# Logits of the latent-attention layer: two heads at a time, the rotary parts in four quadrants of the array

## The chip, the cores and the metric

The kernel runs on one core of a Trainium2 chip. The metric is the device time of one execution in microseconds, as the median of repeated runs; for the kernel before it is 2040.04 us (three runs, 2040.04 to 2044.45). The profile is taken in an execution of its own.

## The reference, cut to what matters

Four layers follow each other on 256 tokens of width 2048: a state-space layer, an attention layer with forget gates ("fox"), a latent-attention layer ("mla") and a second state-space layer ("s5"). The change is in the third one:

```python
def mla_mixer(h, positions, w_in, q_norm, kv_norm, w_q_up, w_kv_up, w_out):
    ...
    q = (rms_norm(q_lat, q_norm) @ w_q_up).reshape(bsz, T, H, MLA_NOPE + MLA_ROPE)     # 16 heads, 128 + 64
    kv = (rms_norm(kv_lat, kv_norm) @ w_kv_up).reshape(bsz, T, H, MLA_NOPE + MLA_V)    # 16 heads, 128 + 128
    ...
    q = jnp.concatenate([q[..., :MLA_NOPE], q_pe], axis=-1)
    k = jnp.concatenate([kv[..., :MLA_NOPE], jnp.broadcast_to(k_pe[:, :, None, :], ...)], axis=-1)
    o = causal_block_attention(q, k, kv[..., MLA_NOPE:], (MLA_NOPE + MLA_ROPE) ** -0.5)
    y = o.reshape(bsz, T, MLA_WIDTH) * jax.nn.silu(z)
    return y @ w_out
```

A head's logits are a sum over 192 features: 128 that each head has for itself (the long product) and 64 rotary ones, whose keys all heads share. With 256 tokens, causal, there are three blocks of 128 x 128: queries 0-127 with keys 0-127, queries 128-255 with keys 128-255, and queries 128-255 with keys 0-127.

## The kernel before, in words

Weights come in half tiles by DMA into seven `raw` buffers (L108). ScalarE rounds each to a high part (`whi`, L119), VectorE makes the rest (`wlo`, L120), four buffers of each, and TensorE multiplies in three products (L126 to L128 with the tokens in rows, L212 to L214 with the features in rows). Such a step takes 12 products of L126 to L128 or 24 of L212 to L214, and ends with `C.tick()`, which runs what is due in a queue: `C.defer(n, fn)` puts `fn` n ticks ahead, and what becomes due is issued behind the step's last product.

The third layer's attention goes over four groups of four heads. A group makes the queries `qs` (line `mla_qn`, two steps), the keys `ks` (`mla_kn`, two steps) and the values `V` (two steps) of its four heads. Between them the queue brings the heads' softmax: `soft` of head c comes 1 + c ticks behind the keys; its `turn` (the transposes of the probabilities, L436, tile `pT`) two ticks later, and its `values` (L444, L445, tile `o`) one tick after that. `soft` calls `logits`: for each of the three blocks d the long product (L897: 128 features of the head) and the 64-row product (L898: rows 0-63 or 64-127 of `qpe` and `kpe`, by the head's parity) into one of four auxiliary PSUM banks, tile `lps`. VectorE evicts it with scale and mask (L900, L902, tile `lg`), takes the maxima (L415, L416) and the negated maxima (L422); ScalarE makes the exponentials (L425, L426, tile `pr`); VectorE divides (L428 to L430). Matrix products are of type float32, each of them two instructions on TensorE; `lg` has two buffers.

Two other places serve for comparison. The second layer's logits (L726 to L728) are three long products per head without a rotary part. The last layer sends 64x64 products into quadrants of the array: L1287 and L1399 use four quadrants in turn, L1383 two.

Of the kernel before, what the change touches and what calls it, by code (L numbers as in the profile page):

```python
# [11 lines left out]
F32 = mybir.dt.float32  # L12
# [3 lines left out]
ALU = mybir.AluOpType  # L16
# [3 lines left out]
P = 128  # L20
# [759 lines left out]
def mla(C, hT, out):  # L780
    nc, A = C.nc, C.A
    H, R, NR = 16, 64, 512
    mm = nc.tensor.matmul
    with C.tc.tile_pool(name="mla", bufs=1) as mp, C.tc.tile_pool(name="mla_w", bufs=1) as wp, C.tc.tile_pool(name="mla_t", bufs=2) as tp:
        C.lt = tp
        mask = C.causal(mp)
# [72 lines left out]
        kpe = mp.tile([P, T], F32, name="kpe")  # L859
# [15 lines left out]
        qpe = mp.tile([P, 8, T], F32, tag="lat", name="qpe")  # L875
        for s in range(2):
            ps = C.proj_tok([A["mla_qr"][s, 0]], latT[0])
            for t in range(2):
                qr = tp.tile([P, 8, R], F32, tag="qr", name="qr")
# [6 lines left out]
        yT = C.new_hT()  # L886
        sc = (P + R) ** -0.5

        def head(h, q, k, V):
            b = 64 * (h % 2)  # L890
            qr, kr_ = qpe[b:b + 64, h // 2], kpe[b:b + 64]

            def logits():
                lps = C.aux("lps")
                for d, qt, kt in ((0, 0, 0), (1, 1, 1), (2, 1, 0)):
                    o, a, e = lps[:, d * P:(d + 1) * P], slice(qt * P, (qt + 1) * P), slice(kt * P, (kt + 1) * P)
                    mm(o, q[:, a], k[:, e], start=True, stop=False)  # L897
                    mm(o, qr[:, a], kr_[:, e], start=False, stop=True)  # L898
                lg = tp.tile([P, 384], F32, tag="lg", name="lg")
                nc.vector.scalar_tensor_tensor(lg[:, 0:256], lps[:, 0:256], sc, mask.rearrange("p a b -> p (a b)"),  # L900
                                               op0=ALU.mult, op1=ALU.subtract)
                nc.vector.tensor_scalar(lg[:, 256:384], lps[:, 256:384], sc, None, op0=ALU.mult)  # L902
                return lg

            def finish(o):
                y = tp.tile([P, T], F32, tag="yf", name="yf")
                nc.vector.scalar_tensor_tensor(y, o[:, 0:T], 0.5, zs[h], op0=ALU.mult, op1=ALU.mult)
                C.split(yT[0][h], yT[1][h], y)

            return C.attend(logits, lambda: V[0], h % 4, finish)  # L910

        for g in range(4):
            qs, ks, Vs = [], [], []
            for nm, l, dst in (("mla_qn", 0, qs), ("mla_kn", 1, ks)):
                for c, ps in enumerate(C.proj_Tk([A[nm][g, 0]], latT[l])):
                    s = tp.tile([P, T], F32, tag=nm, name=nm, bufs=5)
                    nc.scalar.copy(s, ps)
                    dst.append(s)
            for c in range(4):
                C.defer(1 + c, head(4 * g + c, qs[c], ks[c], Vs))  # L920
            V = wp.tile([P, 2, 512], F32, tag="Vg", name="Vg", bufs=2)
            Vs.append(V)
            for t, ps in enumerate(C.proj_tok([A["mla_v"][g, 0]], latT[1])):
                nc.scalar.copy(V[:, t], ps)
# [540 lines left out]
SCAN_US = 1.9  # L1465
LAT_STRIPS = (364, 362, 362)
LAYERS = {0: ssd, 1: fox, 2: mla, 3: s5}


# [99 lines left out]
```

## Time and profile before

| | us |
|---|---|
| median of three runs | 2040.04 |
| the profiled execution | 2042.04 |
| its span on the core | 2040.2 |
| TensorE busy | 1988.5 |
| VectorE busy | 1472.4 |
| ScalarE busy | 957.6 |

The profile comes from one execution. The busy time of an engine is the union of its instructions' spans; a matrix product's span goes on until its result is through, so the spans overlap, and the time from one start (or end) to the next tells what a product costs. The chain of waits lists each piece by the time that it adds behind the piece before.

### The profile page before, as it was taken

To read this page: it belongs to the slowest core of one execution; us is meant where nothing else is said; L and a number is where in the kernel's file an instruction comes from. 1 tells how busy PE (TensorE), PEld (TensorE's weight loads), DVE (VectorE), ACT (ScalarE), POOL (GpSimd) and SP (SyncE) were. 2 spreads that over 40 slices of the span, in tenths; PEclk is the share of its full clock that TensorE was granted. 3 is DMA by queue.
4 is the path that set the end of the run, shared out by engine and by line. 5 is a ranking of instruction groups with operands and counts; after the bars stand their busy time and mean duration, and the time that the engine had idled before them with its cause. 6 is when DMAs were issued, how large, how long until landed. Compare 5 with 4: busy or idle time off the path is not lost.

```text
span 2040.2 us, 31823 instructions
## 1 busy us (share of the span) xinstructions
PE 1988.5 (97%) x12073; PEld 1695.5 (83%) x12073; DVE 1472.4 (72%) x2572; ACT 957.6 (47%) x1427; POOL 409.7 (20%) x482
## 2 busy tenths in 40 slices
PE   8999999999999999999999999999999999999997
PEld 6788888888888878788888879888888799778885
DVE  6798887887644695677776567766556678996856
ACT  5455555555433334344444444545554355445542
POOL 0101111001100018999991000000000000110002
PEclk9999999999999999999999999999999999999999
DMA  8555555555665547565666555654347556685652
GB/s 285 186 184 181 185 176 184 186 185 185 218 200 191 181 139 242 182 205 198 197 209 197 180 183 150 205 190 145 104 145 252 174 184 197 171 250 194 196 191 91
DMA packets 116233, 382.40 MB, mean 187 GB/s; under 512 B 18208, under 2 KB 20976, under 8 KB 114288
## 3 DMA queue, kind: packets, MB, share of 16 engines
q1 hardware_dynamic: 103424, 348.11, 52.5%
q0 software_dynamic: 7808, 26.56, 4.2%
q10 hardware_dynamic: 4848, 5.70, 0.8%
q8 instruction: 95, 1.56, 0.3%
q14 instruction: 58, 0.48, 0.1%
HBM read 366.20 MB, written 14.11 MB: 186 GB/s over the span
## 4 chain that ended last, share of the span: by engine, by line
PE 82%; DVE 10%; DMA 3%; POOL 2%; issue 2%; ACT 1%; SPq 0%; DVEq 0%; POOLq 0%; ACTq 0%
PE pT L147 24%; PE pT L148 12%; PE pt L127 10%; PE pt L126 10%; PE pt L128 10%; DVE wlo L120 3%; PE pk L212 2%; PE pk L214 2%; PE pk L213 2%; PE yd L602 1%; PE lps L898 1%; PE lps L897 1%; DVE hres L339 1%; DVE hres L340 1%; PE o L444 1%
## 5 line engine op out<-in xcount | busy, mean ns | idle before, releaser
L120 DVE TENSOR_TENSOR wlo<-raw,whi 128x1024 fp32r<-128x1024 f32 (+4 forms) x612 | 751.5, 1230 | 340.4 <-ACT whi L119 336.4
L119 ACT CAST whi<-raw 128x1024 fp32r<-128x1024 f32 (+4 forms) x612 | 632.0, 1036 | 730.9 <-PE pt L128 316.9
L147 PE MATMUL pT<-h,whi 128*128 128x512 f32 (+2 forms) x2080 | 744.8, 401 | 0.0
L148 PE MATMUL pT<-h,wlo 128*128 128x256 f32 (+2 forms) x2080 | 585.4, 281 | 3.0 <-DVE wlo L120 3.0
L147 PEld LDWEIGHTS pT<-h,whi 128*128 128x128 f32 (+2 forms) x2080 | 389.6, 187 | 92.8 <-issue 0.2
L148 PEld LDWEIGHTS pT<-h,wlo 128*128 128x128 f32 (+2 forms) x2080 | 392.2, 189 | 4.8 <-DVE wlo L120 3.8
L126 PE MATMUL pt<-whi,h 128*128 128x512 f32 (+2 forms) x716 | 281.0, 393 | 6.5 <-ACT whi L119 6.1
L127 PE MATMUL pt<-wlo,h 128*128 128x512 f32 (+2 forms) x716 | 279.3, 390 | 5.4 <-DVE wlo L120 5.3
L128 PE MATMUL pt<-whi,h 128*128 128x512 f32 (+2 forms) x716 | 276.6, 386 | 0.3 <-DVE h L357 0.3
L127 PEld LDWEIGHTS pt<-wlo,h 128*128 128x128 f32 x716 | 135.9, 190 | 35.2 <-DVE wlo L120 8.4
L126 PEld LDWEIGHTS pt<-whi,h 128*128 128x128 f32 x716 | 135.5, 190 | 34.5 <-ACT whi L119 6.5
L128 PEld LDWEIGHTS pt<-whi,h 128*128 128x128 f32 x716 | 135.8, 190 | 26.9 <-issue 1.7
L589 POOL TENSOR_TENSOR xs<-xs,dsk 128x512 f32<-128x512 f32 x16 | 20.8, 1318 | 372.6 <-ACT xs L585 372.6
L126 PE MATMUL pt<-whi,yh 128*128 128x512 f32 x240 | 95.5, 398 | 0.0
L127 PE MATMUL pt<-wlo,yh 128*128 128x512 f32 x240 | 95.4, 397 | 0.0
L128 PE MATMUL pt<-whi,yl 128*128 128x512 f32 x240 | 94.9, 395 | 0.0
L147 PE MATMUL pT<-y,whi 128*128 128x512 f32 x256 | 90.0, 395 | 0.0
L1166 POOL DMA_DIRECT2D mats<-W_d x8 | 4.3, 539 | 355.6 <-DVE h L292 285.3
L148 PE MATMUL pT<-y,wlo 128*128 128x256 f32 x256 | 72.2, 282 | 0.0
L496 DVE SCALAR_TENSOR_TENSOR conv<-u,cw,conv 128x255 f32<-128x255 f32 x144 | 69.0, 480 | 2.2
L89 POOL MEMSET mask<- 128x256 f32 x2 | 0.6, 314 | 301.3 <-PE pt L128 164.4
L147 PEld LDWEIGHTS pT<-y,whi 128*128 128x128 f32 x256 | 48.3, 189 | 10.7 <-DVE y L292 0.3
(469 smaller groups left out, 3093.4 us busy)
## 6 DMA issues: line engine op xcount, KB each, us to landing
raw<-in_ssd_x SPq DMA_DIRECT2D x64, 512.0 KB
raw<-in_ssd_o SPq DMA_DIRECT2D x64, 512.0 KB
raw<-in_ssd_z SPq DMA_DIRECT2D x63, 512.0 KB
raw<-in_fox_v SPq DMA_DIRECT2D x32, 512.0 KB
raw<-in_fox_q SPq DMA_DIRECT2D x32, 512.0 KB
raw<-in_fox_k SPq DMA_DIRECT2D x32, 512.0 KB
raw<-in_fox_z SPq DMA_DIRECT2D x32, 512.0 KB
raw<-in_fox_o SPq DMA_DIRECT2D x32, 512.0 KB
```

The source lines that it names most:

```text
L119: nc.scalar.copy(hi[:, c], r[:, c])
L120: nc.vector.tensor_tensor(lo[:, c], r[:, c], hi[:, c], op=ALU.subtract)
L126: mm(ps, s[0], m[0], start=first, stop=False)
L127: mm(ps, s[0], m[1], start=False, stop=False)
L128: self.last = mm(ps, s[1], m[0], start=False, stop=last).ins
L147: mm(ps, hi, hT[2][order[kb]], start=kb == 0, stop=False)
L148: self.last = mm(ps[:, 0], lo, hT[0][order[kb]], start=False, stop=kb == KB - 1).ins
L212: mm(o, ws[0], a[0], start=kb == 0 and c % 2 == 0, stop=False)
L213: mm(o, ws[0], a[1], start=False, stop=False)
L214: self.last = mm(o, ws[1], a[0], start=False, stop=end).ins
L496: nc.vector.scalar_tensor_tensor(c[:, k:], u[:, 0:T - k], cw[:, ti, 3 - k:4 - k], c[:, k:], op0=ALU.mult, op1=ALU.add)
L589: nc.gpsimd.tensor_tensor(heads(xs[c]), heads(xs[c]), bc(dsk, g), op=ALU.mult)
```

## The change

`logits2` makes the logits of heads h and h + 1 together, in two PSUM tiles `lps0` and `lps1`. First come the six long products, three for each head. Then the rotary parts of both heads: each 64-row product is cut in two by its queries (64 of the 128 columns of the array), so that a product takes one quadrant: rows 0-63 for head h and 64-127 for head h + 1, output rows 0-63 or 64-127 by m. For each block d the four quadrants follow each other. Then VectorE evicts both tiles. `pair` does this in the even head's turn, runs that head's softmax at once and defers the odd one's by a tick. Pairs come at 1 and 3 ticks behind the keys, so that each head's softmax, transposes and values keep their ticks.

```diff
+        def logits2(h, q, k, lg):
+
+            lps = [C.aux("lps0"), C.aux("lps1")]
+            for i in range(2):
+                for d, qt, kt in BLOCKS:
+                    mm(lps[i][:, part(d)], q[i][:, part(qt)], k[i][:, part(kt)], start=d == 0, stop=False)
+            for d, qt, kt in BLOCKS:
+                for i, m in ((0, 0), (1, 1), (0, 1), (1, 0)):
+                    rows, out = slice(64 * i, 64 * i + 64), slice(64 * m, 64 * m + 64)
+                    mm(lps[i][out, part(d)], qpe[rows, h // 2, qt * P + 64 * m:qt * P + 64 * m + 64], kpe[rows, part(kt)],
+                       start=False, stop=d == 2)
+            for i in range(2):
+                t = lg[i] = tp.tile([P, 384], F32, tag="lg", name="lg")
+                nc.vector.scalar_tensor_tensor(t[:, 0:256], lps[i][:, 0:256], sc, mask.rearrange("p a b -> p (a b)"),
                                                op0=ALU.mult, op1=ALU.subtract)
...
+            return C.attend(lambda: lg[h % 2], lambda: V[0], h % 4, finish)
+
+        def pair(h, q, k, V):
+            lg = {}
+            logits2(h, q, k, lg)
+            head(h, lg, V)()
+            C.defer(1, head(h + 1, lg, V))
...
-            for c in range(4):
-                C.defer(1 + c, head(4 * g + c, qs[c], ks[c], Vs))
+            for c in (0, 2):
+                C.defer(1 + c, lambda h=4 * g + c, q=qs[c:c + 2], k=ks[c:c + 2], V=Vs: pair(h, q, k, V))
```

In the changed kernel the long products stand in L899, the quadrant products in L903, the evictions in L907 and L909, the copies of V in L937.

On TensorE, behind the first step of the first group's V, the kernel before has (the alternation goes on for three products of each line, then a step of V, then the next head):

```order
L128 MATMUL pt1_13403<-whi_13406,ll1_12277 128x512
L897 MATMUL lps_13422<-mla_kn_13393,mla_qn_13323 128x128
L898 MATMUL lps_13422<-kpe_12297,qpe_13112 128x128
...
L126 MATMUL pt0_13402<-whi_13447,lh1_12276 128x512
...
L897 MATMUL lps_13463<-mla_kn_13395,mla_qn_13325 128x128
L898 MATMUL lps_13463<-kpe_12297,qpe_13112 128x128
...
L212 MATMUL pk0_13488<-lh0_12256,whi_13492 128x256
```

and the changed kernel at the same place on TensorE:

```order
L128 MATMUL pt1_13403<-whi_13406,ll1_12277 128x512
L899 MATMUL lps0_13422<-mla_kn_13393,mla_qn_13323 128x128 x3
L899 MATMUL lps1_13423<-mla_kn_13395,mla_qn_13325 128x128 x3
L903 MATMUL lps0_13422<-kpe_12297,qpe_13112 64x128
L903 MATMUL lps1_13423<-kpe_12297,qpe_13112 64x128
...
L126 MATMUL pt0_13402<-whi_13463,lh1_12276 128x512
```

The second head's long products have moved up by one step, and the alternation with the 64-row products is gone; the last two rows before the step stand six times.

On VectorE, at the first pair of the first group, the kernel before has:

```order
L900 SCALAR_TENSOR_TENSOR lg<-lps,mask 128x256
L902 TENSOR_SCALAR lg<-lps 128x128
L415 TENSOR_REDUCE mx<-lg 128x1
L428 RECIPROCAL rc<-sm 128x2
L416 TENSOR_REDUCE mx<-lg 128x1
L429 TENSOR_SCALAR pr<-pr,rc 128x128
L430 TENSOR_SCALAR pr<-pr,rc 128x256
L422 TENSOR_SCALAR nb<-mx 128x2
L120 TENSOR_TENSOR wlo<-raw,whi 128x1024
```

(this is the second head's eviction, with the first head's division behind it) and the changed kernel for both heads:

```order
L907 SCALAR_TENSOR_TENSOR lg<-lps_13422,mask 128x256
L909 TENSOR_SCALAR lg<-lps_13422 128x128
L907 SCALAR_TENSOR_TENSOR lg<-lps_13423,mask 128x256
L909 TENSOR_SCALAR lg<-lps_13423 128x128
L415 TENSOR_REDUCE mx<-lg 128x1
...
L428 RECIPROCAL rc<-sm 128x2
L429 TENSOR_SCALAR pr<-pr,rc 128x128
L430 TENSOR_SCALAR pr<-pr,rc 128x256
...
L120 TENSOR_TENSOR wlo<-raw,whi 128x1024
```

The division of the first head no longer stands behind the eviction of the second head's logits of a later step, and the weight split L120 has gone behind both softmaxes.

## Rows read from the trace of the kernel before

**Rows 1.** The page's first part: busy us (share of the span) and instructions.
```profile
PE 1988.5 (97%) x12073; PEld 1695.5 (83%) x12073; DVE 1472.4 (72%) x2572; ACT 957.6 (47%) x1427; POOL 409.7 (20%) x482
```

**Rows 2.** Busy time by stretch: length, engines, granted clock, DMA share, GB/s.
```profile
1395.00:1520.00 125.00, 125.00 (x771) 106.58 (x770) 71.80 (x182) 64.00 (x157) 0.00 (x0) 1.00 0.38 120
1520.00:1630.00 110.00, 106.56 (x474) 86.50 (x473) 73.36 (x106) 43.35 (x48) 2.18 (x6) 0.98 0.63 214
1630.00:1740.00 110.00, 110.00 (x1375) 105.29 (x1374) 87.19 (x177) 55.94 (x100) 6.59 (x12) 1.00 0.59 185
...
1850.00:1950.00 100.00, 100.00 (x565) 87.36 (x564) 79.57 (x123) 51.68 (x76) 0.00 (x0) 1.00 0.60 189
```

**Rows 3.** Chain of waits, 1402 to 1411 us: start, us added, what.
```profile
1402.78 0.22 PE lps L897 x2
1403.00 0.42 PE lps L898 x2
1403.42 0.42 PE lps L897 x2
1403.83 0.41 PE lps L898 x2
...
1405.08 0.43 PE pt L126
...
1405.98 0.23 PE pt L126
...
1410.34 0.32 PE pk L212
1410.66 0.12 PE pk L213
```

**Rows 4.** Instructions of a tile or line: count, ns (min/median/max), shape.
```profile
L897 PE MATMUL lps<-mla_kn,mla_qn x96: 270/275/377, 1402.6 to 1512.7; 128*128 128x128 f32 x96
L898 PE MATMUL lps<-kpe,qpe x96: 272/322/373, 1402.9 to 1513.2; 64*128 64x128 f32 x96
...
L1287 PE MATMUL vp<-xu,mats x512: 218/218/267, 1644.7 to 1728.6; 64*64 64x64 f32 x171
```

**Rows 5.** Chain of waits in the second layer, first of three like products.
```profile
840.81 0.22 PE lps L726 x2
```

**Rows 6.** Chain of waits in the last layer, around L1287.
```profile
1644.76 1.09 PE vp L1287 x64
1645.85 0.32 PE pk L212
1646.17 0.12 PE pk L213
```

**Rows 7.** Chain of waits in the last layer, around L1383 and L1399.
```profile
1737.33 1.02 PE near L1383 x30
...
1738.41 0.93 PE far L1399 x62
```

**Rows 8.** VectorE in order of time: start, us, line, what [idle before].
```profile
1403.89 1.23 DVE L120 TENSOR_TENSOR wlo<-raw,whi 128x1024 fp32r<-128x1024 f32 x1 [1.63 <-ACT whi L119]
1405.19 0.42 DVE L900 SCALAR_TENSOR_TENSOR lg<-lps,mask 128x256 f32<-128x256 f32 x1
1405.53 0.28 DVE L902 TENSOR_SCALAR lg<-lps 128x128 f32<-128x128 f32 x1
...
1411.69 0.35 DVE L430 TENSOR_SCALAR pr<-pr,rc 128x256 f32<-128x256 f32 x1
1411.96 0.16 DVE L422 TENSOR_SCALAR nb<-mx 128x2 f32<-128x2 f32 x1
...
1435.60 0.42 DVE L900 SCALAR_TENSOR_TENSOR lg<-lps,mask 128x256 f32<-128x256 f32 x1 [0.32 <-PE lps L898]
...
1438.40 0.35 DVE L430 TENSOR_SCALAR pr<-pr,rc 128x256 f32<-128x256 f32 x1
```

**Rows 9.** ScalarE in order of time, first head of the first group.
```profile
1407.39 0.59 ACT L924 COPY Vg<-pt 128x512 f32<-128x512 f32 x1 [3.53 <-PE pt L128]
1407.87 0.40 ACT L425 ACTIVATE pr<-lg,nb 128x128 f32<-128x128 f32 x1
```

**Rows 10.** Chain of waits at the step that uses the split of 1403.89.
```profile
1422.22 0.31 PE pk L212
```

More of the change, by code (lines that the diff above doesn't have):

```diff
@@ L887, in mla, with part, head @@
         sc = (P + R) ** -0.5
[L889 to L900, printed above, removed]
+        BLOCKS = ((0, 0, 0), (1, 1, 1), (2, 1, 0))
+        def part(t):
+            return slice(t * P, (t + 1) * P)
+        def logits2(h, q, k, lg):
[11 more added lines that the diff above has]
+                nc.vector.scalar_tensor_tensor(t[:, 0:256], lps[i][:, 0:256], sc, mask.rearrange("p a b -> p (a b)"),
                                                op0=ALU.mult, op1=ALU.subtract)
-                nc.vector.tensor_scalar(lg[:, 256:384], lps[:, 256:384], sc, None, op0=ALU.mult)
-                return lg
+                nc.vector.tensor_scalar(t[:, 256:384], lps[i][:, 256:384], sc, None, op0=ALU.mult)
+        def head(h, lg, V):
             def finish(o):
@@ L908, in finish @@
                 C.split(yT[0][h], yT[1][h], y)
-            return C.attend(logits, lambda: V[0], h % 4, finish)
+            return C.attend(lambda: lg[h % 2], lambda: V[0], h % 4, finish)
[4 more added lines that the diff above has]
+            C.defer(1, head(h + 1, lg, V))
         for g in range(4):
```

## The prediction

> **What bounds the kernel now.** I began with the page, since it says which engine is full: TensorE is busy 97% of the 2040.2 us span, VectorE 72% [rows 1]. Then the busy time by stretch. The third layer's attention runs from about 1395 to 1520 us; there TensorE is busy for all of the 125 us at full clock, VectorE for 71.80, ScalarE for 64.00, and the DMA engines for 0.38 of the time [rows 2]. No wait of TensorE is on record in that stretch, so a microsecond taken off its stream there is a microsecond off the kernel, until something else comes late.
>
> The chain of waits then shows what TensorE pays for a head's logits [rows 3]. It lists each product by the time that it adds behind the one before. The first long product (L897) takes 0.22 us, then the 64-row and the long products alternate at 0.41 to 0.42 us each, and the first projection behind them takes 0.43 us where the same line takes 0.23 a little later; where the projections of the other kind follow, it is 0.32 against 0.12. Each of the two lines has 96 instructions of some 0.27 us, two for a product, 48 products [rows 4]. The second layer makes the same three long products without a 64-row part between them, and they take 0.22 us each [rows 5]. So a product costs 0.22 us of its own, and each change between a 128-row and a 64-row product some 0.20 us more. One head has three products of each kind and six changes: 2.30 us from the first product to the projection, and 0.20 behind it, together 2.50. A pair costs 5.00, the 16 heads 40 us, of which 16 x 6 x 0.20 = 19 us are changes.
>
> **What the change does to that stream.** Per pair it removes twelve products, of which six are long and six 64-row ones, with twelve changes: 5.00 us. It adds:
>
> *Six long products in a row*, lines and operands as before: 6 x 0.22 = 1.32 us [rows 5].
>
> *Twelve 64x64 products* with 128 moving columns, in two instructions each, 24 in all, spread over four quadrants of the array: rows 0-63 into one PSUM tile, rows 64-127 into the other, the output's upper and lower half by turns. The trace of before has no such block with 128 columns, but the last layer has one with 64: L1287 sends 64 instructions of 64x64 with 64 columns, also in turn over four quadrants with one PSUM tile for each half of the rows [rows 4, 6]. Between two projections they take 1.09 us, and the projection behind them 0.32 instead of 0.12, so 1.29 us. A 128-column instruction takes 0.11 us by [rows 5], so a 64-column one 0.055; four at once make 64 x 0.055 / 4 = 0.88 us, and 0.41 is left for going in and coming out, close to twice the 0.20 above. That the quadrants work at once is borne out by a second block: 62 instructions of L1399, again over four quadrants, in 0.93 us, 15 ns each, while L1383, which uses two quadrants, has 30 in 1.02, 34 ns each with its way in [rows 7].
>
> So 24 instructions with 128 columns take 24 x 0.11 / 4 = 0.66 us if four go at once, and 24 x 0.11 = 2.64 if they go one by one. I take 0.66, the nearest row being L1287's, and keep 2.64 as the other end. With one way in and out at 0.41, the pair costs 1.32 + 0.66 + 0.41 = 2.39 us, against 5.00. That is 2.61 us for a pair and 8 x 2.61 = 20.9 us for the layer.
>
> *VectorE and ScalarE.* No instruction is added or taken away on them, but the odd head's logits are made one turn of the queue earlier, and both heads are evicted together. The transposes of the probabilities (L436) keep their places: two turns behind the logits for the even head, three for the odd one. What shrinks is the time between. Before, two projection steps and another head's logits lay between a head's logits and its transpose; now for the even head it is two projection steps alone, 12 x 0.23 + 24 x 0.12 = 5.6 us [rows 3]. The softmax must be through in that time. In the trace, a chain without anything in between runs from the eviction's start at 1435.60 to the last scaling at 1438.40 + 0.35 = 1438.75, 3.15 us; the second head's eviction adds at most 0.42 + 0.28 = 0.70, and I allow as much for its maxima, so 4.5 us [rows 8]. The order of the changed kernel has VectorE's next weight split (1.23 us) behind the first pair's softmax. In the second pair it stands ahead of the reciprocal, which makes 5.8 us; but there two value products and a transpose lie between as well as two steps of 24 x 0.12. ScalarE has both heads' exponentials ahead of the copies of V, one of which held the first exponential until 1407.87 before [rows 9]. So this costs nothing in my sum. If the cover were gone, TensorE would stand at L436, and the projections behind it too.
>
> *Weight splits.* They come up to one turn later on VectorE. The four buffers of each half hide that: the split at 1403.89 is for projections that TensorE only reaches at 1422.22 [rows 8, 10]. *DMA.* The weight loads keep their order, and 120 GB/s in this stretch becomes some 145, against 214 in the next one [rows 2]. *PSUM.* A pair takes two of the four auxiliary banks at once; the ones that it reuses were evicted a turn earlier. I price all three at nothing.
>
> **Sum.** The profiled execution took 2042.04 us, its span 2040.2 and 1.84 around it; 2042.04 - 20.9 = 2021.1. The median of the runs shown is 2040.04, 2.0 below that execution, so the median after is forecast at 2040.04 - 20.9 = 2019.1 us. Nothing later takes it back: from 1520 us on TensorE is the full engine in most stretches [rows 2], and its later waits are for engines that are shifted with it.
>
> **Rivals.**
> *Two quadrants at once, not four.* The two instructions of a product use one quadrant and stand behind each other. If a later instruction can't start ahead of an earlier one that still waits for its quadrant, the second half of a product overlaps only the first half of the next. The quadrant block then takes 24 x 0.11 / 2 = 1.32 us, the pair 3.05, the gain is 8 x 1.95 = 15.6 us and the time 2024.4. For it: 128 columns hold a quadrant twice as long as in [rows 6]. Against it: under this rule L1287's block would have taken 64 x 0.055 / 2 = 1.76 us and its ways in and out, and it took 1.29 with both. The Trainium skill ("TensorE: Matmul & The Clock Gate", Part 3: Packing small matmuls) has matmuls start and end strictly in program order; by that rule this rival would be the forecast. The block of L1287 does not agree with it when each product's two instructions stand together.
>
> *The softmax is late.* The longest chain in the trace, from the first eviction at 1405.19 to the end of the scaling at 1411.69 + 0.27 = 1411.96, is 6.77 us [rows 8]; with the second head's eviction 7.5. Against the 5.6 us available TensorE would wait 1.9 us in each pair, 15 us in all, and 5.9 us would be left: 2034.1. For it: VectorE is 57% busy there and gets more crowded. Against it: that chain was long because the exponential stood behind the copy of V and the reciprocal behind the next head's logits, and neither is so in the changed order.
>
> *One by one.* The quadrants don't overlap: 1.32 + 2.64 + 0.41 = 4.37 us for a pair, 8 x 0.63 = 5.0 us gained, 2035.0. This is the change not doing what it says. [rows 6] and [rows 7] stand against it.
>
> *A drain at each change of quadrant, so slower.* Every quadrant product could pay what each 64-row product pays now, 0.42 us [rows 3]: 12 x 0.42 = 5.04, with 1.32 and the way out 0.20 it is 6.56 for a pair, 1.56 more than now, 12.5 us in all: 2052.5. It decides from (5.00 - 1.32 - 0.20) / 12 = 0.29 us for a product on. For it: four-way use with accumulation onto what 128-row products left in the bank is not in the trace. Against it: L1287's products come at 2 x 1.09 / 64 = 0.034 us each.
>
> **Chances.** Four at once, gain near 20.9: 0.82. Two at once: 0.09. Late softmax: 0.03. One by one: 0.03. Drains: 0.03. My own case spreads from 2016.5 (half of the 0.41 hidden, 1.6 us, and 1 us of scatter between runs) to 2022; the two-at-once case is at 2024.4, so the range goes to 2025.5 and leaves out the rest. About 0.3%, 6.1 us, is what a measurement here can tell from no change. The first two cases are faster by more than that, the next two are within it, the last is slower: faster 0.91, same 0.06, slower 0.03.
>
> **What the profile after would show.** L899 and L903 in the chain: per pair 12 long instructions at 0.11 us, and from the first L903 to the projection some 0.9 us at 15 to 30 ns for an instruction; the projection behind them 0.20 longer than its like. The stretch from the first logits to the output projection is shorter by about 21 us, with TensorE still full. Two at once shows as L903 at about 55 ns for an instruction; a late softmax as idle TensorE ahead of L436, released by the scaling of pr. A gain under 15 us, or a wait that is new behind 1500 us, would prove my sum wrong.

## The result, and the profile after

The changed kernel takes 2020.01 us (median of four runs, 2014.97 to 2021.63) against 2040.04, 20.0 us less; the forecast was 2019.1 us. The measured ratio is 0.9889, with an interval of 0.9875 to 0.9903; the quotient of the two medians, 0.9902, lies within it. The profiled execution took 2021.63 us, where 2021.1 was forecast, with a span of 2019.8, which is 20.4 under the span before. The four runs scatter by 6.7 us, so a median within 1 us of the forecast is partly luck; TensorE's own stream is the closer test.

The chain of waits at the first pair shows the new stream; its rows answer to [rows 3] (start, us added, what).

```profile
1406.02 1.34 PE lps L899 x12
1407.36 0.82 PE lps L903 x24
1408.18 0.43 PE pt L126
1408.61 0.24 PE pt L127
1408.84 0.23 PE pt L128
1409.08 0.23 PE pt L126
...
1415.55 0.81 PE lps L903 x24
1416.37 0.32 PE pk L212
1416.68 0.12 PE pk L213
```

Twelve long instructions add 1.34 us, 0.11 each as in the second layer. The 24 quadrant instructions add 0.82, and the projection behind them is 0.20 longer than its like, with either kind of projection. A pair costs 1.34 + 0.82 + 0.20 = 2.36 us where it cost 5.00. All eight pairs show 1.34 and 0.81 or 0.82, so the stream is 8 x 2.64 = 21.1 us shorter. The instructions themselves have about kept their spans (against [rows 4]; count, ns, shape):

```profile
L903 PE MATMUL lps<-kpe,qpe x192: 269/269/321, 1407.3 to 1491.4; 64*64 64x128 f32 x192
L899 PE MATMUL lps<-mla_kn,mla_qn x96: 272/275/275, 1405.9 to 1490.6; 128*128 128x128 f32 x96
```

There are 48 more products than before in the layer's logits, counted by 192 + 96 instructions against 96 + 96, each with about as long a span, and yet less time: what shrank is the distance between them. Here neither an engine's instruction count nor the sum of its spans tells its time.

The stage is as full as before. The row of busy time by stretch (length, then TensorE, weight loads, VectorE, ScalarE, GpSimd, granted clock, DMA share, GB/s) answers to the first of [rows 2]:

```profile
1395.00:1499.60 104.60, 104.60 (x882) 95.86 (x881) 72.06 (x184) 64.67 (x160) 0.00 (x0) 1.00 0.44 145
```

TensorE is busy for all of it at full clock, VectorE has the same 72 us of work in less time, and the weights come at 145 GB/s in place of 120. No wait of TensorE stands in the stretch. Where VectorE waited 19.0 us in 14 waits for `lps`, it now waits 0.5 in 3 (who waited for whom: us, times, longest; before, then after):

```profile
DVE lg L900 <- PE lps L898: 19.0, 14, 3.8
DVE lg L907 <- PE lps L903: 0.5, 3, 0.2
```

From the first logits to the last value product (L445) it was 1402.6 to 1524.2, 121.6 us, and is 1405.9 to 1506.2, 100.3 us: 21.3 less. The stage began 3.2 us later in this execution, behind work that is the same in both kernels. Over all eleven profiled executions the first long product comes between 1400.5 and 1406.0 us, so its start scatters by more than that. The stretch behind the stage gave 2.4 us back; among the waits there the one for `mats` fell from 3.7 to 2.3 us. The causes of both were not looked for.

VectorE in order of time at the first pair answers to [rows 8]: start, us, line, what.

```profile
1408.30 0.42 DVE L907 SCALAR_TENSOR_TENSOR lg<-lps,mask 128x256 f32<-128x256 f32 x1
1408.64 0.28 DVE L909 TENSOR_SCALAR lg<-lps 128x128 f32<-128x128 f32 x1
1408.84 0.41 DVE L907 SCALAR_TENSOR_TENSOR lg<-lps,mask 128x256 f32<-128x256 f32 x1
...
1411.69 0.35 DVE L430 TENSOR_SCALAR pr<-pr,rc 128x256 f32<-128x256 f32 x1
```

The even head's probabilities are ready at 1412.04, 3.74 us behind the eviction's start. The chain has TensorE at its transposes (L436) from 1413.88 on. Over all eight pairs the even head takes 3.74 to 4.31 us, and its probabilities are ready at least 1.7 us before the first transpose starts. ScalarE's exponentials and copies of V stand in the order that the forecast relied on:

```profile
1410.27 0.40 ACT L425 ACTIVATE pr<-lg,nb 128x128 f32<-128x128 f32 x1 [3.16 <-DVE nb L422]
...
1412.04 1.04 ACT L937 COPY Vg<-pt 128x512 f32<-128x512 f32 x2
```

### The profile page after: what moved, and what is told of

The parts are those of the page before. It is cut to its first block, busy times and chain, and to the rows that moved or that the text cites. A ratio compares the mean times of both kernels' runs of the same rounds, so it can differ in the third digit from the quotient of the medians.

```text
span 2019.8 us, 32021 instructions
## 1 busy us (share of the span) xinstructions
PE 1970.5 (98%) x12169; PEld 1684.2 (83%) x12169; DVE 1470.2 (73%) x2572; ACT 956.4 (47%) x1427; POOL 410.1 (20%) x482
## 4 chain that ended last, share of the span: by engine, by line
PE 82%; DVE 10%; DMA 3%; POOL 2%; issue 2%; ACT 1%; SPq 0%; DVEq 0%; POOLq 0%; ACTq 0%
PE pT L147 24%; PE pT L148 12%; PE pt L127 10%; PE pt L128 10%; PE pt L126 10%; DVE wlo L120 3%; PE pk L212 2%; PE pk L214 2%; PE pk L213 2%; PE yd L602 1%; DVE hres L339 1%; DVE hres L340 1%; PE o L444 1%; DMA raw<-in_ssd_z 1%; PE kp L1077 1%
## 5 line engine op out<-in xcount | busy, mean ns | idle before, releaser
L120 DVE TENSOR_TENSOR wlo<-raw,whi 128x1024 fp32r<-128x1024 f32 (+4 forms) x612 | 749.5, 1227 | 350.1 <-ACT whi L119 343.7
```

The source lines that it names most:

```text
L120: nc.vector.tensor_tensor(lo[:, c], r[:, c], hi[:, c], op=ALU.subtract)
```

## The experiments

Theory A is that of the forecast: a change between products of 128 and of 64 rows costs TensorE some 0.2 us, and products on different parts of the array run at once, so that the rotary block is bound by its moving columns. The rivals say that the overlap of the quadrants alone made the gain, that the cost belongs to something else than the height, or that fewer than four quadrants work at once. Each time was compared with runs of the kernel before on the same chip; the intervals are 3 to 5 us wide on either side, so the chain of waits decides between neighbours, and the time only checks it. The expectations count times from 2040 us; in these runs the kernel before took 2041.85 to 2043.86, so gains should be compared, not times. The gains in time differ from what the chains add up to by -2.0 to +3.8 us.

**One head at a time, grouped.** The kernel before with one edit:

```diff
-                for d, qt, kt in ((0, 0, 0), (1, 1, 1), (2, 1, 0)):
-                    mm(o, q[:, a], k[:, e], start=True, stop=False)
-                    mm(o, qr[:, a], kr_[:, e], start=False, stop=True)
+                for f in range(2):
+                    for d, qt, kt in ((0, 0, 0), (1, 1, 1), (2, 1, 0)):
+                        if f == 0:
+                            mm(o, q[:, a], k[:, e], start=d == 0, stop=False)
+                        else:
+                            mm(o, qr[:, a], kr_[:, e], start=False, stop=d == 2)
```

> The kernel before with one edit: within each head the three long products come first and the three 64-row products behind them; one head at a time, no quadrants, nothing moved between heads. Theory A (each change of height costs about 0.2 us): two changes in place of six, a head takes 0.66 + 0.66 + 0.40 = 1.72 us against 2.50, 16 x 0.78 = 12.5 us gained, 2027.5 us. Rival (the alternation is free, and the gain came from the overlap of quadrants alone): 2040 us.

2028.87 us against 2043.08, ratio 0.9938 (0.9916 to 0.9961). Its chain:

```profile
1400.99 0.67 PE lps L899 x6
1401.65 0.86 PE lps L901 x6
1402.52 0.43 PE pt L126
1402.95 0.23 PE pt L127
```

0.67 + 0.86 + 0.20 = 1.73 us for a head, where it was 2.50: theory A's 1.72. The products are the same in number, size and operands; only their order and their flags for the start and end of an accumulation differ, and four of six changes are gone. So the changes cost 0.19 to 0.20 us each, and these four alone make 16 x 0.77 = 12.3 of the 21.1 us. The rival that gave all to the quadrants falls.

The other 8.8 us are 1.10 for each pair: two heads so grouped take 3.46 us, the changed kernel's pair 2.36. Of that, 0.66 is overlap (twelve 64-row instructions at 0.11 us take 1.32, the quadrant block 0.66), and the rest is that a pair pays the way in and out once, where two heads pay it twice. Overlap so makes 5.3 us of the gain, and all changes saved together 15.8.

The weight loads (PEld) of the kernel before show where a change costs its time:

```profile
1402.39 0.42 PEld L897 LDWEIGHTS lps<-mla_kn,mla_qn 128*128 128x128 f32 x2
1402.93 0.29 PEld L898 LDWEIGHTS lps<-kpe,qpe 64*128 64x128 f32 x2
```

L897's first weights start to load at 1402.39, just as the product ahead of it starts, and 0.23 us before its own product does. L898's do not load ahead: they start at 1402.93, together with their own product and 0.20 us behind the start of the last L897 instruction (1402.73). In the grouped kernel, instructions of one height start 0.112 us apart; the first one behind a change starts 0.205 behind its predecessor and the second 0.213 behind the first, together 0.19 more. Why the weights of the other height are not loaded ahead is not shown.

**Both heads in quadrants, block by block.** Two long products, then four quadrant products, three times:

```diff
-            for i in range(2):
-                for d, qt, kt in BLOCKS:
+            for d, qt, kt in BLOCKS:
+                for i in range(2):
                     mm(lps[i][:, part(d)], q[i][:, part(qt)], k[i][:, part(kt)], start=d == 0, stop=False)
-            for d, qt, kt in BLOCKS:
                 for i, m in ((0, 0), (1, 1), (0, 1), (1, 0)):
```

> Both heads together and in quadrants as in the changed kernel, but block by block: two long products, four quadrant products, three times. Theory A: six changes of height in a pair in place of two, four more at 0.16 to 0.20 us, 0.7 us in each of 8 pairs, 5.8 us, 2025.8 us. Rival (changes cost nothing when the quadrants are full): 2020 us.

2025.81 us against 2043.08, ratio 0.992 (0.9901 to 0.9939). Its chain:

```profile
1404.04 0.45 PE lps L899 x4
1404.48 0.38 PE lps L902 x8
1404.86 0.64 PE lps L899 x4
1405.50 0.38 PE lps L902 x8
...
1406.90 0.43 PE pt L126
```

Four long instructions take 0.45 us behind a projection and 0.64 behind quadrants, a change of 0.19; eight quadrant instructions take 0.38, that is 0.22 for themselves and 0.16 for the change. A pair takes 3.07 us, 0.71 more than the changed kernel, as theory A had it: changes cost much the same, 0.16 to 0.19 us, when the quadrants are full.

**No product of 64 rows.** The rotary keys stand in two tiles with zeros in the other head's rows:

```diff
+        kz = mp.tile([P, 2, T], F32, name="kz")
+        nc.gpsimd.memset(kz, 0.0)
+        nc.scalar.copy(kz[0:64, 0], kpe[0:64])
+        nc.scalar.copy(kz[64:128, 1], kpe[64:128])
...
+            for i in range(2):
+                for d, qt, kt in BLOCKS:
+                    mm(lps[i][:, part(d)], qpe[:, h // 2, part(qt)], kz[:, i, part(kt)], start=False, stop=d == 2)
```

> No product of 64 rows at all: the rotary keys stand in two tiles of 128 rows with zeros in the other head's half, and six 128-row products follow the six long ones. Theory A (the 0.2 us belong to the change of height): 24 instructions of 0.11 us in a row, 2.68 us in the chain, no longer projection behind them; against 1.34 + 0.82 + 0.20 = 2.36 us now, 0.32 more in each of 8 pairs, 2022.6 us, that is 17 to 18 us under the kernel before without any quadrant. Rival (the cost belongs to going from one pair of operands to another): the six products cost 0.2 us on the way in and out as before, 3.0 us, 2026 us.

2021.53 us against 2043.86, ratio 0.9891 (0.9875 to 0.9908). Its chain, with the long products on L903 and the padded ones on L906:

```profile
1404.24 1.34 PE lps L903 x12
1405.58 1.34 PE lps L906 x12
1406.92 0.23 PE pt L126
```

The padded products are 128-row products like any other, half of their rows multiply zeros, and there is no way in and none out. A pair costs 2.68 us, 0.32 more than with quadrants. So the cost belongs to the height, not to the change of operands. And most of the gain, 8 x 2.32 = 18.6 us, is to be had without a single quadrant.

**Halves of the rows, no quadrants.** The 64-row products stay whole, the two heads' by turns:

```diff
             for d, qt, kt in BLOCKS:
-                for i, m in ((0, 0), (1, 1), (0, 1), (1, 0)):
+                for i in range(2):
+                    rows = slice(64 * i, 64 * i + 64)
+                    mm(lps[i][:, part(d)], qpe[rows, h // 2, part(qt)], kpe[rows, part(kt)], start=False, stop=d == 2)
```

> The rotary products of a pair stay whole: 64 rows by 128 columns of the array, rows 0-63 for head h and 64-127 for head h + 1, grouped behind the long products; no quadrants. Theory A (a change of height costs about 0.2 us, and parts of the array on different rows work at once, bound by the moving columns): 12 instructions at 0.11 / 2 = 0.66 us with the same way in, so 0.82 us in the chain from the first of them to the next projection, as with quadrants; time 2020 us. Rival (only the cut into quadrants lets products overlap): 12 x 0.11 + 0.16 = 1.48 us in the chain, 0.66 us more in each of 8 pairs, 2025 us.

2019.63 us against 2043.86, ratio 0.988 (0.9865 to 0.9895). Its chain:

```profile
1403.84 0.87 PE lps L903 x12
1404.70 0.43 PE pt L126
```

Twelve instructions in 0.87 us where 24 quadrant ones took 0.82, and where theory A had 0.82 as well. Two halves at once do as well as four quadrants for the block itself, because each product then covers twice the columns of the array: 12 x 0.11 / 2 and 24 x 0.11 / 4 are both 0.66. The 0.05 us lie in the way in: the second instruction of a half starts 213 ns behind the first, that of a quadrant 160, and their weights take some 186 and 133 ns to load. So the cut into quadrants is worth 0.05 us for a pair, 0.4 in all, which no timing here could tell. What the change needed beyond grouping was the pair, not the quadrants.

**The quadrant block twice.** The twelve products are issued a second time (L908), so that the rotary part counts double.

> The block of twelve quadrant products is issued twice for each pair (the rotary part counts double). Theory A (four at once, bound by columns): 24 x 0.11 / 4 = 0.66 us more in each pair, 1.48 us in the chain, 5.3 us in all, 2025.3 us; so the way in is 0.16 us. Rival (the 0.82 us are mostly a fixed way in): under 0.5 us more in each pair, 2023 us or less. Rival (two at once with a way in of near nothing can't be): 1.3 us more, 2030 us.

2025.49 us against 2043.86, ratio 0.9906 (0.9891 to 0.9921). Its chain:

```profile
1402.57 0.81 PE lps L903 x24
1403.39 0.66 PE lps L908 x24
1404.04 0.43 PE pt L126
```

The second block adds 0.66 us, 24 x 0.11 / 4. So four quadrants work at once for the whole block, and 0.16 of the first block's 0.82 is the way in. The starts of the instructions in the changed kernel's trace say the same directly: four start within 20 ns, the next four 160 ns behind the first, and from then on four every 109 ns, in all eight pairs.

**The rotary part left out.** The twelve quadrant products are gone and the logits lack their rotary part.

> The rotary part is left out of the logits; the long products of a pair stay together. Theory A: a pair takes 1.34 us in place of 2.36, 8 x 1.02 = 8.2 us less than the changed kernel, 2011.8 us: what the rotary parts still cost. Rival (the shorter stretch makes the softmax late, and TensorE waits ahead of L436): less than that, with idle time there.

2014.69 us against 2043.08, ratio 0.9865 (0.9847 to 0.9882). The pair's long products take 1.34 us and the projection behind them 0.23, so a pair is 1.02 us shorter than in the changed kernel, 8.2 us in all. The time expected was 2011.8, but from 2043.08 the gain is 28.4 us, 8.4 more than the changed kernel's 20.0. No wait of TensorE is on record in the stage: even with steps that close together the softmax is in time. The rotary parts cost 1.02 us a pair now, and 3.66 before.

**Three other orders of the twelve quadrant products.** The block's cost rests on which quadrant follows which. First, all three products of a quadrant before the next one:

```diff
-            for d, qt, kt in BLOCKS:
-                for i, m in ((0, 0), (1, 1), (0, 1), (1, 0)):
+            for i, m in ((0, 0), (1, 1), (0, 1), (1, 0)):
+                for d, qt, kt in BLOCKS:
```

> The twelve quadrant products of a pair in another order: all three of one quadrant before the next quadrant. Theory A1 (a quadrant's queue is its own, so the order does not matter): 0.82 us in the chain for the 24 instructions, time 2020 us. Rival A2 (instructions start in program order, so a product that waits for its quadrant holds back those behind it): nearly one at a time, 24 x 0.11 less three seams, about 2.3 to 2.6 us in the chain, 8 x 1.6 = 13 us more, 2033 us.

2025.68 us against 2043.86, ratio 0.9908 (0.9888 to 0.9928). The chain has 1.62 us, between both expectations (its row counts 22 of the 24 instructions):

```profile
1402.10 1.62 PE lps L903 x22
1403.71 0.43 PE pt L126
```

Two further orders were to tell whether each half of the rows has a stream of its own:

```diff
+            for i, d, m in [(i, d, m) for i in range(2) for d in range(3) for m in range(2)]:
```

> Quadrant products in another order: head h's six first (rows 0-63, the output half by turns), then head h + 1's six (rows 64-127). It asks what held the order of one quadrant at a time at 1.6 us. Theory A3 (each half of the rows has its own stream, in program order within it): the halves still run beside each other, 0.82 us in the chain, time as the changed kernel. Rival A4 (one stream for all, in which a product that waits for its quadrant lets only a few behind it pass): the two halves run one after the other, two quadrants at once, 24 x 0.11 / 2 + 0.16 = 1.5 us, 8 x 0.65 = 5 us more.

and

```diff
+            for i, d, m in [(i, d, (m + i) % 2) for m in range(2) for d in range(3) for i in range(2)]:
```

> Quadrant products in another order: the halves of the rows by turns from product to product, but each stays in one quadrant for three products and then takes the other (head h in the upper, head h + 1 in the lower half of the output, then the other way). Theory A3 (a stream for each half of the rows, in program order within it): in a half six instructions of one quadrant, 0.66 us, then six of the other, less one seam, 1.2 us and 0.16 for the way in, 1.4 us in the chain, 4.5 us more in all. Rival A1 (every quadrant has its own stream): 0.82 us. Rival A4 (one stream, few may pass): 1.5 us, so it is told from A3 by the other run.

Their times are 2024.79 against 2041.85, ratio 0.9913 (0.9889 to 0.9937), and 2023.69 against 2041.85, 0.9914 (0.9888 to 0.994). In the chain both have the same row; this one is of the first:

```profile
1401.86 1.08 PE lps L903 x24
1402.95 0.43 PE pt L126
```

1.08 us in both orders fits none of the three expectations: separate streams for the halves wanted 0.82 and 1.4, a stream for each quadrant 0.82 twice, and one stream with little passing 1.5 twice. That both are alike says that halves of the rows and halves of the output count the same.

The starts of the single instructions in the traces show more. (The records do not name the quadrant, but the starts fall into series 109 ns apart, and the first instruction of each series has a span of 320 ns, the others 269.) In ns from the block's first start, and within 2 ns alike in all eight pairs:

- One quadrant after the other: the first quadrant's six instructions start at 0, 160, 269, 378, 487 and 596, and the first ones of the next three quadrants at 275, 550 and 825. So a quadrant begins while two instructions of the one ahead, its last product, still wait, and passes them.
- Two quadrants at a time: six instructions start in each, as above, and the first ones of the other two quadrants at 282 and 289. They pass four waiting instructions, the last product of each of the two quadrants ahead.

Each time the next quadrant begins 2 or 3 ns after the weights of the fourth of the six instructions ahead start to load. The last start is then at 617 ns by turns, 885 in two blocks and 1421 in four; 0.20 us behind it ends the chain's piece, which gives the 0.82, 1.08 and 1.62 us. So products do pass others that wait for their quadrant, but only a few: what fits all three orders is at most two waiting instructions, one product, for each quadrant, while a fixed number over all quadrants does not fit both two and four. By turns from product to product no quadrant is left without work. Whether the limit counts instructions, products or weight loads stays open.

## Why the prediction was right

- *TensorE is the bound, so its stream is the time:* right. The stream became 21.1 us shorter, the stage 21.3, the span 20.4 and the median 20.0.
- *A change of height costs 0.20 us:* right, and shown apart from everything else. Grouping within a head removed four of six and saved 0.77 us; padding removed all of them.
- *Six long products at 0.22 us:* 1.32 us forecast, 1.34 measured.
- *Quadrants, 0.66 for the block and 0.41 for both ways:* 0.66 by the doubled block; 0.16 in and 0.20 out, 0.36. The estimate from the last layer's block of 64 columns held at 128. Its small miss was in dividing L1287's 1.29 us: the fours there start 58 ns apart, so the 64 instructions take 0.93 and not 0.88, and 0.36 was left for the ways in and out, not 0.41. The pair was forecast at 2.39 us and took 2.36.
- *Nothing new comes late:* right for the order chosen. The softmax took 3.74 us in the first pair where I had allowed 4.5: only one of the second head's two maxima comes ahead of the first head's exponential. In the first group's second pair, with the split ahead of the reciprocal, it took 4.31 where I had allowed 5.8. The weight splits cost nothing.
- *Two quadrants at once:* this rival falls by the doubled block and by the starts in fours. The Trainium skill's rule that matmuls start strictly in program order ("TensorE: Matmul & The Clock Gate", Part 3: Packing small matmuls) does not agree with the trace here. With a product's two instructions together it would have 1.32 us for the 24 instructions that took 0.66; and in the order of one quadrant after the other, the second quadrant starts at 275 ns, ahead of two instructions of the first at 487 and 596. The orders that stay in a quadrant show a limit to the passing, though, so the rule is not without a core.
- *Late softmax, one by one, a drain at each change of quadrant:* none of them appeared. The late softmax was summed with a last scaling of 0.27 us, where its row has 0.35; so it comes to 6.85 us in place of 6.77, which changes nothing.

What the forecast did not ask is which part of the change was needed. It priced 0.66 us for the block in quadrants and would have priced the same for the two halves of the rows: 12 x 0.11 / 2. That was there to be worked out.

## What to carry to other kernels

Where products of 128 and of 64 rows alternate on TensorE, look at the distance between starts, not at spans: 0.42 us for a product that costs 0.22 in a row of its like was the whole finding here. Group by height first, which alone took 12 of the 21 us; then let neighbours share the array, by rows or by quadrants, in turn from product to product, which also pays the change of height once for both; and where the heights can be made equal with zeros, that comes within 0.3 us a pair of the best. When a change has two parts, price each alone before giving the credit to the one that looks cleverer.

## What the runs showed that I had not expected

The order within the quadrant block matters by up to a factor of two: 0.82 us by turns, 1.08 in two blocks, 1.62 in four, for the same 24 instructions. And splitting a 64-row product into two quadrants, with twice the instructions and weight loads, cost nothing and gained next to nothing: 0.82 against 0.87 us.
